# Hybrid attention and pooling layer: half of the output projection moved into the attention loop

## The chip, the cores and the metric

The kernel runs on one core of one Trainium2 chip. The metric is the device time of one execution in microseconds (us), a median over runs. The profile is that of one further execution; its span runs from the first to the last instruction on the core.

## The reference, cut to what matters

One layer over 2048 tokens of width 1024, float32. Half of the mixed width (512) is attention with eight heads of 64, the other half a pooled branch:

```
z = rmsnorm(x) @ w_in                    # q, k, v, u
att  = dilated_attention(q, k, v)        # 8 heads, three (window, dilation) patterns
pool = multiscale_pool(u)                # 4 groups of 128 channels
h = x + concat([att, pool]) @ w_out      # the output projection
h = h + (silu(gate) * val) @ w_down      # gated MLP, depthwise conv before the activation
h = h + sigmoid(rmsnorm(h) @ w_gate) * (p @ w_ple)
return rmsnorm(h)
```

So `h1 = x + att @ w_out[:512] + pool @ w_out[512:]`. The pooled half needs nothing of attention.

## The kernel before, in words

Everything is kept transposed: 128 channels on the partitions, tokens along the free axis, in four chunks of 512 tokens. A float32 product is made of float32r parts: each operand is split into a high part `hi` and the rest `lo`, and three matmuls (hi·hi, hi·lo, lo·hi) stand for one (`mm3`, lines 89 to 91). The program has four phases, one behind the other on TensorE: the input projection (`phase_project`, up to 397 us of the profile), attention (`phase_attention`, 397 to 724 us), the output projection (the first part of `phase_rest`, 724 to 926 us), and then the MLP and the gated embedding.

**Attention** runs 128 steps: 8 heads of 16 query tiles of 128 tokens, two heads being a pair. `CFG["ord"]` is the order in which each engine's work of a step is written: every pair is a stage and its lag in steps. `N` and `F` are the near and far scores on TensorE (lines 572 and 561), `nm` and `fm` bias and minimum on VectorE, `ne` and `fe` the exponentials on ScalarE, `T` the transposes of the weights (line 600), `h` and `l` their split on ScalarE and VectorE, `V` and `W` the products with the values, six steps later, into the one bank `o`. After two such steps the bank is emptied: `o` copies half of it on ScalarE (`ev`), `p` adds the other half on VectorE into `s1` or `s3` (line 660). Only then may the next `V` write it. `perm` is the order of the four query tiles in a group of four steps; a tile with a larger index has more far keys, and more blocks to transpose. Behind each of the first three pairs, `M` mixes its branches on GpSimd and its own DMA queue: weights are broadcast from DRAM (`wb`, line 891), products, split and stores of `mh` and `ml`. The order on TensorE, ScalarE, VectorE and GpSimd is as written; on SyncE (SP), which issues most loads, the planner sets it.

For each head, `load_qk` fetches queries and keys. An operand tile has 128 partitions, the 64 rows of a head twice: `qhh` holds the high part of q in both halves, `qll` the low part in both, `ks` the high part of k above its low part. These are six loads of 64 rows of 8 KB, 512 KB each:

```
for half in range(2):
    hs = slice(half * DH, half * DH + DH)
    loads.append((t.qhh[hs], g.qh[pr][rows]))
    loads.append((t.ks[hs], (g.kh if half == 0 else g.kl)[pr][rows]))
    loads.append((t.qll[hs], g.ql[pr][rows]))
```

The loads of head h+1 are issued one per step from the second step of head h on. PSUM has eight banks: one for near scores, two for far scores, two tiles of two banks for the transposes (`tp`), one for `o`.

**The output projection** goes chunk by chunk. For each of its 8 output tiles the sum over 8 row blocks of `w_out` is 24 matmuls of 512 columns; the pooled blocks are 4 to 7. Then the residual is added (line 1231, VectorE), `h1` is stored, and the square sum for the next norm is taken. In chunks 2 and 3 small pieces of the MLP's preparation, a list `todo`, are worked off on VectorE and ScalarE, one behind the matmuls of each row block and group of four tiles.

Of the kernel before, what the change touches and what calls it, by code (L numbers as in the profile page):

```python
# [43 lines left out]
CFG = {"tt": 2, "ee": 2, 'ord': [['B', 0], ['M', 0], ['N', 0], ['S', 1], ['o', 7], ['F', 0], ['h', 2], ['nm', 0], ['p', 7], ['fm', 0], ['l', 2], ['T', 1], ['V', 6], ['W', 6], ['ne', 0], ['fe', 0]], 'perm': [3, 2, 1, 0], 'fp': [[0], [1], [2], [3]], 'np': [[0, -1], [1], [2], [3]], 'm': [9, 10, 13, 4, 6, 7]}  # L44
# [125 lines left out]
def phase_project(tc, g, xT, w_in, pool_w, rcnt):  # L170
# [4 lines left out]
    with ExitStack() as ctx:  # L175
# [116 lines left out]
        for c, (t0, n) in enumerate(chunks):  # L292
# [3 lines left out]
            for gi, grp in enumerate((0, 1, 2, 3) if not final else (0, 1, 3, 2)):  # L296
# [58 lines left out]
                for j in range(nt):  # L355
# [16 lines left out]
                    elif grp == 1:  # L372
# [3 lines left out]
                        rdma(nc, residues(g.kh[j], t0, n), hi)  # L376
                        rdma(nc, residues(g.kl[j], t0, n), lo)
# [108 lines left out]
def phase_attention(tc, g, mx, near_b, far_b):  # L486
# [4 lines left out]
    NS = H * NQ  # L491
    with ExitStack() as ctx:
# [3 lines left out]
        ps_t = ctx.enter_context(tc.tile_pool(name="b_t", bufs=2, space=PSUM, reuse_waits="tile"))  # L496
        ps_o = ctx.enter_context(tc.tile_pool(name="b_o", bufs=1, space=PSUM, reuse_waits="tile"))

        heads, steps, groups, pairs = {}, {}, {}, {}

        def load_qk(h):
# [23 lines left out]
        def load_v(pr, which, q):  # L525

            v = sb.tile([P, 4, 2, P], F32R, tag=which, bufs=4 + (which == "v1"), name=f"{which}_{pr}_{q}")
# [5 lines left out]
        V_STEPS = {n: (("v3", "v1")[x], q) for x in range(2) for q, n in enumerate(((24, 28, 32, 36), (19, 30, 34, 38))[x])}  # L533

        def begin(s):
# [16 lines left out]
            st.tt = sb.tile([P, 768], F32, tag="tt", bufs=CFG["tt"], name="tt")  # L552
            st.ee = sb.tile([P, 768], F32, tag="ee", bufs=CFG["ee"], name="ee")

# [150 lines left out]
        def mix(s):  # L705
            for pr in range(NPAIR - 1):
# [9 lines left out]
                for c in range(NCH):  # L716
                    if d == CFG["m"][2] + CFG["m"][3] * c:
                        mix_fetch(nc, g, mx, nc.gpsimd, pr, pairs[pr], c)
                    if d == CFG["m"][2] + CFG["m"][3] * c + CFG["m"][4]:
                        mix_products(nc, g, mx, nc.gpsimd, pairs[pr], c)  # L720
                    if d == CFG["m"][2] + CFG["m"][3] * c + CFG["m"][5]:
                        mix_store(nc, g, mx, nc.gpsimd, nc.gpsimd, pr, pairs[pr], c)()

        near_bank = []
        sel = mx.tile([8, NCH, 2, DH], F32R, tag="sel", name="sel")
        for c in range(NCH):
            nc.vector.tensor_copy(sel[:, c], g.ident[:8, c : 8 : NCH, None].to_broadcast([8, 2, DH]))
        with tc.manual_schedule(engines=set(EN.values())):
            for dst, src in load_qk(0):
                rdma(nc, dst, src)  # L730
            for q in range(4):
# [5 lines left out]
                "T": turn, "h": high, "l": low, "V": values, "W": values_b, "S": stats, "M": mix, "o": fold, "p": folded, "B": begin  # L737
            }
            for s in range(NS + 10):
                if s < NS:  # L740
# [5 lines left out]
                    for pr in range(1, NPAIR):  # L746
                        if s - 2 * NQ * (pr - 1) in V_STEPS:
                            rdma(nc, *load_v(pr, *V_STEPS[s - 2 * NQ * (pr - 1)]))
                if s == NS + 2:
                    last_far(nc, g, mx, ps_t, pairs[NPAIR - 1])  # L750
                    pieces = pairs[NPAIR - 1].pieces = last_weights(nc, mx, pairs[NPAIR - 1])
                for nm, lag in CFG["ord"]:
                    if 0 <= s - lag < NS or nm == "M":
# [7 lines left out]
def mix_stats(nc, g, sb, psum, pr, pt):  # L761
# [8 lines left out]
    sy = sb.tile([16, CH], F32, tag="sy", name="sy")  # L770
# [23 lines left out]
def last_near(nc, g, sb, psum, pt):  # L794
# [9 lines left out]
    pt.near = [sb.tile([16, CH], F32, tag="sy", name="nr")[:8], sb.tile([P, CH], F32, tag="m3", bufs=1, name="nr")[:8]]  # L804
# [4 lines left out]
def last_far(nc, g, sb, psum, pt):  # L809
# [5 lines left out]
    pt.far = [sb.tile([8, CH], F32, tag="fr", bufs=2, name="fr") for _ in range(2)]  # L815
# [4 lines left out]
def last_weights(nc, sb, pt):  # L820

    both = (pt.near, pt.far)
    lo = sb.tile([P, CH], F32, tag="m1", bufs=1, name="lo")[:8]
# [71 lines left out]

# [1076 lines left out]
```

## Time and profile before

| | us |
|---|---|
| median of 3 runs (2460.84 to 2463.77) | 2463.16 |
| the profiled execution: its span | 2454.4 |
| time of the median run around that span | 8.8 |
| first near score to last near score (128 steps) | 397.7 to 706.4 |
| chunk 0 of the output projection | 724 to 800 |
| chunks 1 to 3 | 800 to 926 |

The trace names an instruction by engine, source line and tiles, `out<-in`. "PE" is TensorE, "DVE" VectorE, "ACT" ScalarE, "POOL" GpSimd; "PEld" is a weight load. The DMA share is the busy share of the core's 16 DMA engines. q0 is the queue that GpSimd issues to ("software_dynamic" in the profile), q1 that of SP ("hardware_dynamic").

### The profile page before, as it was taken

Reading aid. Unit: us, or ns where it says so; the run is one execution under the profiler, and the core shown is the slowest. Engines: PE = TensorE matmul, PEld = TensorE weight load, DVE = VectorE, ACT = ScalarE, POOL = GpSimd, SP = SyncE. Lnnn points to the kernel's source line nnn. Section 1 sums busy time; section 2 is a strip of 40 time slices with the busy share of each in tenths; the row PEclk is TensorE's granted clock in tenths of the full one; section 3 lists DMA queues with packets and bytes.
Section 4 is the critical chain, followed back from the end, with each engine's and each line's share of the span. In section 5 each row is a group of like instructions: output and inputs, shape, how many; then the busy total and the mean of one; then the engine's idle time right before and its main releaser. Section 6 shows DMA issues by size and latency. Waiting matters only on the chain.

```text
span 2454.4 us, 32544 instructions
## 1 busy us (share of the span) xinstructions
PE 2345.7 (96%) x11251; PEld 1970.6 (80%) x11251; DVE 1723.2 (70%) x2705; ACT 1146.1 (47%) x2055; POOL 547.3 (22%) x552
## 2 busy tenths in 40 slices
PE   8999999888879999999999999999999999999998
PEld 7888887787767887888888787788878888888888
DVE  6645437787774367999999989877766565755655
ACT  5423326787761125445445545444445444543332
POOL 3312221044340023344332366100020000000100
PEclk9999999898989999999999999999999999999999
DMA  7535448878747576456566778544388676654332
GB/s 240 175 133 185 146 153 249 178 173 193 181 142 260 189 253 202 161 187 211 192 197 219 260 275 272 197 145 142 125 287 287 226 255 206 215 176 158 125 100 91
DMA packets 248516, 476.06 MB, mean 194 GB/s; under 512 B 47744, under 2 KB 74176, under 8 KB 245280
## 3 DMA queue, kind: packets, MB, share of 16 engines
q1 hardware_dynamic: 199376, 385.20, 49.7%
q0 software_dynamic: 29328, 61.02, 7.4%
q10 hardware_dynamic: 19648, 27.77, 3.3%
q8 instruction: 88, 1.44, 0.3%
q14 instruction: 76, 0.62, 0.1%
HBM read 313.08 MB, written 160.73 MB: 193 GB/s over the span
## 4 chain that ended last, share of the span: by engine, by line
PE 73%; DVE 10%; DMA 7%; issue 4%; ACT 2%; POOL 0%; DVEq 0%; POOLq 0%; ACTq 0%; SPq 0%
PE ua L1319 15%; PE uc L1319 8%; PE dn L90 5%; PE dn L89 5%; PE dn L91 5%; PE ub L1319 4%; PE z L91 4%; PE z L89 4%; PE z L90 4%; PE o L89 2%; PE o L91 2%; PE o L90 2%; PE gp L89 2%; PE gp L90 2%; PE gp L91 2%
## 5 line engine op out<-in xcount | busy, mean ns | idle before, releaser
L90 PE MATMUL dn<-al,wu 128*128 128x512 f32 x616 | 240.1, 390 | 4.7 <-DVE al L85 4.7
L89 PE MATMUL dn<-ah,wu 128*128 128x512 f32 x616 | 240.1, 390 | 0.0
L91 PE MATMUL dn<-ah,wu 128*128 128x512 f32 x616 | 239.8, 389 | 0.0
L85 DVE TENSOR_TENSOR al<-ra,ah 128x512 fp32r<-128x512 f32 x154 | 105.8, 689 | 114.1 <-ACT ah L84 110.7
L89 PE MATMUL z<-hnh,wh 128*128 128x512 f32 (+1 forms) x480 | 169.9, 354 | 9.5 <-ACT hnh L252 6.0
L90 PE MATMUL z<-hnl,wh 128*128 128x512 f32 (+1 forms) x480 | 169.7, 354 | 3.4 <-DVE hnl L253 3.3
L91 PE MATMUL z<-hnh,wl 128*128 128x512 f32 (+1 forms) x480 | 169.6, 353 | 2.3 <-POOL wl L85 1.7
L84 ACT CAST ah<-ra 128x512 fp32r<-128x512 f32 x154 | 95.2, 621 | 148.2 <-PE dn L91 130.6
L90 PEld LDWEIGHTS dn<-al,wu 128*128 128x128 f32 x616 | 115.6, 188 | 30.0 <-DVE al L85 6.2
L85 DVE TENSOR_TENSOR wu<-ru,wu 128x1024 fp32r<-128x1024 f32 x88 | 136.5, 1551 | 2.4 <-ACT wu L84 2.4
L89 PEld LDWEIGHTS dn<-ah,wu 128*128 128x128 f32 x616 | 115.6, 188 | 24.3 <-ACT ah L84 0.2
L91 PEld LDWEIGHTS dn<-ah,wu 128*128 128x128 f32 x616 | 115.6, 188 | 23.9
L1319 PE MATMUL uc<-a22h,wu 128*128 128x512 f32 x352 | 116.9, 393 | 3.4 <-DVE uv L1342 3.4
L1319 PE MATMUL ua<-s1h,wu 128*128 128x512 f32 x352 | 115.8, 390 | 3.0 <-ACT ug L1546 3.0
L1319 PE MATMUL ub<-a12h,wu 128*128 128x512 f32 x352 | 117.0, 393 | 0.7 <-ACT a12h L1375 0.6
L1319 PE MATMUL ua<-s2h,wu 128*128 128x512 f32 x352 | 115.9, 390 | 0.9 <-ACT ug L1520 0.7
L1319 PE MATMUL ua<-s4h,wu 128*128 128x512 f32 x352 | 115.7, 389 | 0.5 <-ACT uv L1567 0.5
L1319 PE MATMUL uc<-s3h,wu 128*128 128x512 f32 x352 | 115.6, 389 | 0.0
L1319 PE MATMUL ua<-a11h,wu 128*128 128x512 f32 x352 | 115.5, 389 | 0.0
L85 DVE TENSOR_TENSOR wu<-rw,wu 128x512 fp32r<-128x512 f32 x149 | 101.0, 687 | 17.3 <-ACT wu L84 17.3
L89 PEld LDWEIGHTS z<-hnh,wh 128*128 128x128 f32 x480 | 94.0, 196 | 21.5 <-ACT hnh L252 6.0
L155 DVE TENSOR_TENSOR acc<-acc,sq 128x512 f32<-128x512 f32 (+1 forms) x125 | 81.1, 649 | 42.0 <-ACT sq L154 28.5
(336 smaller groups left out, 6670.3 us busy)
## 6 DMA issues: line engine op xcount, KB each, us to landing
ru<-in_w_up_dram SPq DMA_DIRECT2D x66, 512.0 KB, 4.1
wr<-in_w_in_dram SPq DMA_DIRECT2D x64, 256.0 KB, 4.2
rw<-in_w_down_dram SPq DMA_DIRECT2D x61, 256.0 KB, 4.0
nt<-h SPq DMA_DIRECT2D x56, 256.0 KB, 3.8
td<-t SPq DMA_DIRECT2D x22, 512.0 KB, 2.6
t<-td SPq DMA_DIRECT2D x22, 512.0 KB, 3.7
nt<-in_w_down_dram POOLq DMA_DIRECT2D x44, 256.0 KB, 5.4
ra<-oq0s SPq DMA_DIRECT2D x44, 256.0 KB, 3.9
```

The source lines that it names most:

```text
L84: nc.scalar.copy(hi, src)
L85: (low or nc.gpsimd).tensor_tensor(lo, src, fp(hi), op=ALU.subtract)
L89: nc.tensor.matmul(ps, wh, ah, start=first, stop=False, skip_group_check=again)
L90: nc.tensor.matmul(ps, wh, al, start=False, stop=False, skip_group_check=again)
L91: nc.tensor.matmul(ps, wl, ah, start=False, stop=last, skip_group_check=again)
L155: nc.vector.tensor_tensor(acc[:, :n], acc[:, :n], sq[:, :n], op=ALU.add)
L1319: nc.tensor.matmul(pst, x[:, ksl], y, start=first and k == 0 and n == 0, stop=k == HK - 1 and n == 2, skip_group_check=True)
```

## The change

The pooled half of chunks 1 to 3, 288 matmuls, moves into the attention loop, into steps 15 to 110. A part is one output tile of one chunk (24 parts), spread over four steps: four matmuls in each of the first three (`X`, line 780 of the new kernel), and in the fourth the addition of the residual on VectorE (`E`, line 788). SP fetches four 128x128 blocks of `w_out` for the next part (`xr`, 256 KB), the tile of `x` (`xx`), and stores the sum to `h1`; GpSimd splits the weights into `xh` and `xl`. The pooled activations of a chunk (`xa`, 2 MB) are loaded ahead. In the output projection chunks 1 to 3 then sum row blocks 0 to 3 alone and read `h1` in place of `x`, and two pieces of `todo` follow each row block instead of one.

The sums of `X` take one PSUM bank. `perm` alternates steps with many and with few transposes, and a step with few takes a one-bank tile `u`: `tp` then has three banks in all in place of four. Scores and exponentials share one tile (`tt` is `ee`), the products of `M` are written over `wb`, and one buffer of values goes. Six loads of a head become three: `kh` and `kl` lie in one DRAM tensor `kk`, and each load fills all 128 partitions from a source that is 2 x 64 rows of 8 KB, for q the same 64 rows twice.

```diff
-            loads = []
-            for half in range(2):
-                hs = slice(half * DH, half * DH + DH)
-                loads.append((t.qhh[hs], g.qh[pr][rows]))
-                loads.append((t.ks[hs], (g.kh if half == 0 else g.kl)[pr][rows]))
-                loads.append((t.qll[hs], g.ql[pr][rows]))
-            loads += [(t.fb, far_b[h]), (t.nb, near_b[h])]
-            return loads
+            both = lambda z: z[pr][None, rows].to_broadcast([2, DH, S])
+            return [
+                (t.qhh, both(g.qh)),
+                (t.ks.rearrange("p c r j -> p (c r j)"), g.kk[pr][:, rows].rearrange("a p c r j -> a p (c r j)")),
+                (t.qll, both(g.ql)),
+                (t.fb, far_b[h]),
+                (t.nb, near_b[h]),
+            ]
...
-            st.tp = ps_t.tile([P, 1024], F32, tag="t", name="tp")
+            if st.nf > 2:
+                st.tp = ps_t.tile([P, 1024], F32, tag="t", name="tp")
+            else:
+                st.tp = ps_t.tile([P, CH], F32, tag="u", name="tp")
...
+        def fill_loads(s):
+            u, j = divmod(s - FILL, 4)
...
+            if 0 <= u + 1 < len(parts) and j == 0:
+                held["raw"] = mx.tile([P, 4, P], F32, tag="xr", name="xr")
+                o = parts[u + 1][1]
+                nc.sync.dma_start(held["raw"], w_out[4 * P :, o * P : (o + 1) * P].rearrange("(k p) n -> p k n", p=P))
+            if 0 < u <= len(parts) and j == 0:
+                c, o = parts[u - 1]
+                nc.sync.dma_start(g.h1[o][:, c * CH : (c + 1) * CH], fills.pop(u - 1).x)
+            if 0 <= u < len(parts):
+                c, o = parts[u]
+                if j == 1:
+                    fl = fills[u]
+                    fl.x = mx.tile([P, CH], F32, tag="xx", bufs=2, name="xx")
+                    nc.sync.dma_start(fl.x, xT[o, :, c * CH : (c + 1) * CH])
...
+                if j == 2:
+                    hi = held["next"] = mx.tile([P, CH], F32R, tag="xh", bufs=2, name="xh")
+                    nc.gpsimd.tensor_copy(hi, raw)
+                if j == 3:
+                    hi, lo = held["next"], mx.tile([P, CH], F32R, tag="xl", name="xl")
+                    nc.gpsimd.tensor_tensor(lo, raw, fp(hi), op=ALU.subtract)
...
+            mine = [(k, w, a) for k in range(4) for w, a in ((hi, 0), (hi, 1), (lo, 0))]
+            for n, (k, w, a) in list(enumerate(mine))[4 * j : 4 * j + 4]:
+                nc.tensor.matmul(fills[u].ps, w[:, k * P : (k + 1) * P], acts[c, k][a], start=n == 0, stop=n == 11)
...
+            if 0 <= u < len(parts) and j == 3:
+                fl = fills[u]
+                nc.vector.tensor_tensor(fl.x, fl.ps, fl.x, op=ALU.add)
...
-            mix = {k: load_mix(c, k) for k in ks[:split_at]}
+            kc = ks if c == 0 else ks[4:]
+            mix = {k: load_mix(c, k) for k in kc[:split_at]}
...
-                    if todo:
-                        todo.pop(0)()
+                    for _ in range(2):
+                        if todo:
+                            todo.pop(0)()
...
-                    nc.sync.dma_start(x, xT[4 * grp + j, :, cs])
+                    nc.sync.dma_start(x, g.h1[4 * grp + j][:, cs] if c else xT[4 * grp + j, :, cs])
```

How the loads stand on SP where the fifth head's are issued; `qh`, `kh`, `kl` and `ql` are the DRAM tensors of q and k, the last figures the destination. Before:

```order
L56 DMA qhh_5290<-qh_83 64x2048
L56 DMA ks_5292<-kh_91 64x2048
L56 DMA qll_5291<-ql_87 64x2048
L56 DMA qhh_5290<-qh_83 64x2048
L56 DMA ks_5292<-kl_95 64x2048
L56 DMA qll_5291<-ql_87 64x2048
L56 DMA fb_5294<-in_far_b_dram 128x512
```

The same place in the changed kernel; `h_399` is a tile of `h1`:

```order
L56 DMA qhh_5458<-qh_83 128x1x2048
L56 DMA ks_5460<-kk_91 128x1x2048
L56 DMA qll_5459<-ql_87 128x1x2048
L743 DMA xr<-in_w_out_dram 128x4x128
L746 DMA h_399<-xx 128x512
L56 DMA fb_5462<-in_far_b_dram 128x512
L752 DMA xx<-in_xT_dram 128x512
```

The weights and the `x` tile of two parts now stand on SP's queue right behind the three loads of a head.

One step of attention on TensorE, near scores to values, where `V` begins to write the bank `o`. Before:

```order
L572 MATMUL sn<-ks_4018,qhh_4016 128x256
L573 MATMUL sn<-ks_4018,qll_4017 128x256
L561 MATMUL sf<-ks_4018,qhh_4016 128x512
L562 MATMUL sf<-ks_4018,qll_4017 128x512
L600 MATMUL tp<-ident,ee 128x128 x2
L628 MATMUL o<-pth,v_0_3_3998 128x256
```

In the changed kernel, a group later:

```order
L573 MATMUL sn<-ks_4407,qhh_4405 128x256
L574 MATMUL sn<-ks_4407,qll_4406 128x256
L562 MATMUL sf<-ks_4407,qhh_4405 128x512
L563 MATMUL sf<-ks_4407,qll_4406 128x512
L604 MATMUL tp<-ident,ee 128x128 x3
L780 MATMUL x<-xa1l,xh 128x512
L780 MATMUL x<-xa1h,xl 128x512
L780 MATMUL x<-xa2h,xh 128x512
L780 MATMUL x<-xa2l,xh 128x512
L632 MATMUL o<-pth,v_1_1_4956 128x256
```

The four matmuls stand between the transposes and the values.

VectorE in a fourth step of a part in the changed kernel; `ISA` is the fused bias and minimum:

```order
L621 TENSOR_TENSOR ptl<-tp,pth 128x384
L788 TENSOR_TENSOR xx<-x,xx 128x512
L578 ISA ee,st_3991<-sn,nb_4009 128x256
L578 ISA st_3991 128x1
L664 TENSOR_TENSOR s_3993<-o,ev 64x512
```

The addition of the residual, which needs the load of `xx`, stands ahead of the step's near minimum and of the addition that frees `o`; before, the split (`ptl`) was followed by that minimum directly.

More of the change, by code (lines that the diff above doesn't have):

```diff
@@ L525, in load_v @@
         def load_v(pr, which, q):
[L527 removed]
+            v = sb.tile([P, 4, 2, P], F32R, tag=which, bufs=4, name=f"{which}_{pr}_{q}")
             vals[pr, which, q] = v
@@ L719, in mix, with load_acts @@
                     if d == CFG["m"][2] + CFG["m"][3] * c + CFG["m"][4]:
-                        mix_products(nc, g, mx, nc.gpsimd, pairs[pr], c)
+                        mix_in_place(nc, nc.gpsimd, pairs[pr], c)
                     if d == CFG["m"][2] + CFG["m"][3] * c + CFG["m"][5]:
                         mix_store(nc, g, mx, nc.gpsimd, nc.gpsimd, pr, pairs[pr], c)()
+        parts = [(c, j) for c in range(1, NCH) for j in range(KD)]
+        acts, held, fills = {}, {}, {}
+        def load_acts(c, k):
+            acts[c, k] = [mx.tile([P, CH], F32R, tag=f"xa{k}{a}", name=f"xa{k}{a}") for a in "hl"]
+            for t, m in zip(acts[c, k], (g.mh, g.ml)):
+                rdma(nc, t, m[4 + k][:, c * CH : (c + 1) * CH])
@@ new lines, in fill @@
+        def fill(s):
+            u, j = divmod(s - FILL, 4)
+            if not 0 <= u < len(parts) or j == 3:
+                return
+            c, o = parts[u]
+            if j == 0:
+                fills[u] = Shared()
+                fills[u].ps = ps_x.tile([P, CH], F32, tag="x", name="x")
+            hi, lo = held[u]
+            mine = [(k, w, a) for k in range(4) for w, a in ((hi, 0), (hi, 1), (lo, 0))]
+            for n, (k, w, a) in list(enumerate(mine))[4 * j : 4 * j + 4]:
+                nc.tensor.matmul(fills[u].ps, w[:, k * P : (k + 1) * P], acts[c, k][a], start=n == 0, stop=n == 11)
+            if j == 2:
+                held.pop(u)
@@ L736, in phase_attention @@
                 "F": far_scores, "N": near_scores, "fm": far_max, "nm": near_max, "fe": far_exp, "ne": near_exp,
-                "T": turn, "h": high, "l": low, "V": values, "W": values_b, "S": stats, "M": mix, "o": fold, "p": folded, "B": begin
+                "T": turn, "h": high, "l": low, "V": values, "W": values_b, "S": stats, "M": mix, "X": fill, "E": fill_out, "o": fold, "p": folded, "B": begin
             }
@@ L748, in phase_attention @@
                             rdma(nc, *load_v(pr, *V_STEPS[s - 2 * NQ * (pr - 1)]))
+                fill_loads(s)
+                fill_split(s)
+                if s == NS:
+                    sel = mx.tile([P, CH], F32R, tag="xh", bufs=2, name="sel")[:8].rearrange("p (c e d) -> p c e d", c=NCH, e=2)
+                    for c in range(NCH):
+                        nc.vector.tensor_copy(sel[:, c], g.ident[:8, c : 8 : NCH, None].to_broadcast([8, 2, DH]))
                 if s == NS + 2:
@@ L803, in last_near @@
             )
-    pt.near = [sb.tile([16, CH], F32, tag="sy", name="nr")[:8], sb.tile([P, CH], F32, tag="m3", bufs=1, name="nr")[:8]]
+    pt.near = [sb.tile([P, CH], F32, tag=t, name="nr")[:8] for t in ("xl", "xa1l")]
     for a in range(2):
@@ L814, in last_far @@
             nc.tensor.transpose(out[:, r, :], pt.st3[:, r, a].rearrange("p e i -> p (e i)"), g.ident)
-    pt.far = [sb.tile([8, CH], F32, tag="fr", bufs=2, name="fr") for _ in range(2)]
+    pt.far = [sb.tile([P, CH], F32, tag=t, name="fr")[:8] for t in ("xa0h", "xa0l")]
     for a in range(2):
@@ L918, in mix_store @@
     cs = slice(c * CH, (c + 1) * CH)
-    hi = sb.tile([P, CH], F32R, tag="ah", bufs=3, name="ah")
-    lo = sb.tile([P, CH], F32R, tag="al", bufs=3, name="al")
+    if pr == NPAIR - 1 and c == NCH - 1:
+        hi, lo = (sb.tile([P, CH], F32R, tag=t, name=t) for t in ("xa3h", "xa3l"))
+    else:
+        hi = sb.tile([P, CH], F32R, tag="ah", bufs=2, name="ah")
+        lo = sb.tile([P, CH], F32R, tag="al", bufs=2, name="al")
     mix_split(nc, eng, pt, hi, lo)
@@ L1160, in step, with begin_both, wait @@
                 return [load] + [lambda x=x: (small[x](), small[x + 1]()) for x in range(0, 8, 2)]
-            out = [lambda: begin_one(c0), lambda: begin_one(c0 + 1)]
+            def begin_both():
+                for c in (c0, c0 + 1):
+                    dgs = spread_prep(nc, g, sb, g.pw[c])
+                    todo.insert(len(todo) - 4 * 5 - (c == c0), lambda c=c, dgs=dgs: spread_one(c, dgs))
+            def wait():
+                pass
+            if half:
+                out = [lambda: begin_one(c0), lambda: begin_one(c0 + 1)]
+            else:
+                out = [begin_both] + [wait] * 3
             for k in range(KD // 2):
@@ L1190, in one @@
                     todo.extend(prepare(0, np0, todo))
-            tk.later(4, one)
+            tk.later(2 if c == 1 else 4, one)
         for c in range(NCH):
```

57 lines of the change are left out of this document (34 added, 23 removed).

## The prediction

> **What bounds the kernel now.** I read the page's engine totals, then the stretches of the phases, then attention step by step, and last the DMA queues, since the change gives SP other loads. First the page, engine by engine: busy time, share of the span, instructions.
>
> ```profile
> PE 2345.7 (96%) x11251; PEld 1970.6 (80%) x11251; DVE 1723.2 (70%) x2705; ACT 1146.1 (47%) x2055; POOL 547.3 (22%) x552
> ```
>
> TensorE bounds the kernel, and the change adds and removes no matmul: it can only fill or open gaps of TensorE. Next the stretches that it touches: steps 15 to 110 of attention, chunk 1 of the output projection, chunks 2 and 3. Columns: length, busy time of each engine, granted clock, DMA share, GB/s. Then the near scores with which steps 15 and 111 begin, and those of two steps four apart.
>
> ```profile
> core 0: us, PE busy (x) PEld busy (x) DVE busy (x) ACT busy (x) POOL busy (x), PEclk, DMA share, GB/s
> 428.35:671.85 243.50, 203.76 (x1246) 183.85 (x1246) 187.06 (x559) 193.16 (x533) 75.21 (x79) 0.93 0.79 183
> 800.00:842.00 42.00, 42.00 (x188) 34.81 (x189) 11.51 (x19) 5.29 (x9) 1.04 (x1) 1.00 0.64 206
> 842.00:926.00 84.00, 83.42 (x376) 68.85 (x375) 51.73 (x75) 24.12 (x39) 16.41 (x12) 1.00 0.65 216
> ...
> 428.35 0.28 PE L572 MATMUL sn<-ks,qhh 128*128 128x256 f32 x1
> ...
> 671.85 0.28 PE L572 MATMUL sn<-ks,qhh 128*128 128x256 f32 x1
> ...
> 440.04 0.33 PE L572 MATMUL sn<-ks,qhh 128*128 128x256 f32 x1
> ...
> 448.25 0.33 PE L572 MATMUL sn<-ks,qhh 128*128 128x256 f32 x1
> ```
>
> Chunks 1 to 3 run TensorE without a gap; attention does not. The 96 steps took 243.5 us, 24 groups of four; an undisturbed group took 8.21 us, so 46.5 us are disturbances. What TensorE waited for in these steps (total, times, longest):
>
> ```profile
> PE o L628 <- DVE s L660: 20.5, 24, 5.3
> PE o L642 <- DVE s L660: 10.7, 23, 1.0
> ...
> PE sn L573 <- DMA qll<-ql: 2.6, 1, 2.6
> ```
>
> It is the wait for the emptied bank `o`: 31.2 us in all, 1.3 us a group. So the room is small: the moved matmuls take longer than this (below), and the gap between them and the waits must be paid in attention.
>
> **The change, part by part.** *The matmuls out of the projection.* A row of the chain prices twelve 512-column matmuls, and VectorE's residual addition has its own row:
>
> ```profile
> 964.24 2.72 PE uc L1319 x12
> ...
> L1231 DVE TENSOR_TENSOR xc<-o,xc x32: 679/686/692, 784.0 to 924.7; 128x512 f32<-128x512 f32 x32
> ```
>
> 288 are 24 x 2.72 = 65.3 us, all on the path there: minus 65.3. The cover of VectorE's work goes with them. In chunks 2 and 3 TensorE keeps 84.0 - 43.5 = 40.5 us, VectorE still has 51.7: 11 us become visible, at the bank's release or at the MLP's start. Bounds: 0, if that start waits for nothing of it; 17, if nothing of VectorE's late start in chunk 2 is caught up. I take 11. Net: minus 54.
>
> *The same matmuls in attention.* A group becomes 8.21 + 2.72 us less what they cover. `X` stands ahead of `V` in the step of L628's wait (20.5 us), not in that of L642's, where `E` stands. In an undisturbed group I take 0.4 us as covered: 10.53 us, 24 x 10.53 = 252.7. Of the 46.5 us of disturbances half, 23, since longer steps give the loads that cause them more time: 276, or plus 32 against 243.5. Bounds 252.7 (plus 9) and 299 (plus 56). VectorE (187 us + 24 x 0.69) and ScalarE (193) have room in 276 us, so `E` costs nothing while `xx` is there; if it is late, the near minimum, the freeing of `o` and the next `V` are late behind it.
>
> *GpSimd's splits.* Casting and subtracting 128x512:
>
> ```profile
> 694.35 0.61 POOL L913 CAST ah<-m 128x512 fp32r<-128x512 f32 x1
> 695.04 1.28 POOL L914 TENSOR_TENSOR al<-m,ah 128x512 fp32r<-128x512 f32 x1
> ...
> POOL wb L891 <- issue: 20.5, 3, 8.9
> POOL m L902 <- DMA wb<-wd: 19.5, 5, 13.4
> ```
>
> 1.9 us a group, hidden outside the mixing. In it GpSimd has about 9.0 us for one chunk, so 10.9 against 10.5: 0.4 us over some ten groups, 4 us, inside the bounds above. Its waits (40 us in two rows) were free; now the next part's weights queue behind them: rival D.
>
> *Nothing taken for:* one `tp` of each size (alternating steps reuse a buffer after two steps, as before); the minimum written into `ee` (the transposes that free it stand ahead of the same step's scores on TensorE); products over `wb`, four value buffers, the later `S`, and `sel` (VectorE has 56 us free here; without it, under 1 us each); moved loads and stores of `x`, `h1` and `xa` (25 MB over 276 us, 91 GB/s beside 183, under the 401 below).
>
> *The loads of a head.* This decides. First transfers of one size on one queue, from 688 to 704 us, when little else ran (KB each, median us from issue to landing); then the DMA share in single stretches.
>
> ```profile
> ml<-al POOLq DMA_DIRECT2D x2, 256.0 KB, 3.3
> wb<-wd POOLq DMA_DIRECT2D x2, 256.0 KB, 8.9
> ...
> 684.00:687.00 3.00, 3.00 (x24) 2.98 (x23) 2.35 (x9) 2.62 (x8) 2.82 (x3) 1.00 0.24 90
> 692.40:693.30 0.90, 0.90 (x7) 0.90 (x7) 0.90 (x3) 0.51 (x3) 0.82 (x2) 1.00 0.11 46
> 694.50:696.50 2.00, 1.88 (x15) 1.64 (x13) 1.38 (x5) 1.95 (x6) 1.92 (x3) 1.00 0.30 105
> 697.60:698.10 0.50, 0.50 (x5) 0.50 (x4) 0.45 (x1) 0.50 (x3) 0.50 (x1) 1.00 1.00 401
> 511.00:523.00 12.00, 10.87 (x74) 9.91 (x74) 10.63 (x33) 10.99 (x32) 10.84 (x11) 1.00 0.95 195
> ```
>
> A plain 256 KB store fills all engines (share 1.00, 401 GB/s). `wb` has the same size and takes three times as long: with one left in flight the share is 0.11 of 16, 1.8 engines, at 46 GB/s, 26 GB/s each. Its source is 2 rows broadcast to 64 partitions each: an outermost step of 2. It ran on two engines. The merged loads have just that form, 2 x 64 rows onto 128 partitions; the six old ones, 64 rows, used all engines though at half rate (511 to 523: 0.95, 195 GB/s). No SP load of before has an outermost step under 16, so its queue's behaviour isn't shown; bounds are 2 engines and 16. I take 2, since the form is nearest to `wb`. Price of one, 1.049 MB: at 2 x 26 GB/s 20.2 us (22.4 at the 23.4 GB/s an engine of 684 to 687), three 60.5; at 401 GB/s 2.6, three 7.8.
>
> Which two is the next question. Two `wb` in flight took 0.30 x 16 = 4.8 engines, so that GpSimd's take turns. The page names that queue "software_dynamic" and SP's "hardware_dynamic"; a turn needs a kept state, and I take the same two each time for SP as likelier. The Trainium skill ("DMA: Bandwidth & Descriptors", section "Why a DMA increments its semaphore by 16 and not by 1") says that the largest number up to 16 that divides the outermost counts of both sides sets the engines, on both kinds of queue, and that SP's queue takes the lowest-numbered ones while GpSimd's moves on. The trace agrees for GpSimd's queue (1.8 engines); no run here shows it for SP's. By it the sum is that of the same two, by turns that of rival B.
>
> With the same two, three loads of a head pass one behind the other, and what SP issues behind them has a sixteenth of its bytes on each of these engines, so it lands when they are through. SP's rows at the start, and the first and last near score:
>
> ```profile
> 358.17 0.51 SPq L56 DMA_DIRECT2D qhh<-qh  x1
> ...
> 402.49 0.38 SPq L56 DMA_DIRECT2D v<-vf  x1
> ...
> L572 PE MATMUL sn<-ks,qhh x128: 222/332/562, 397.7 to 706.4; 128*128 128x256 f32 x120, 128*128 128x128 f32 x8
> ```
>
> Head 0: 358.2 + 60.5 + 2.5 (landing; the 3.3 us of `ml` less its data) = 421 in place of 397.7. The values, 4.2 MB, of which a sixteenth at 26 GB/s is 10 us: 429. Head 1: 489. `xa`, the first weights and the biases, 2.75 MB: 6.6 us, 496; landing and GpSimd's split: the first `X`, step 15, at 500 instead of 428. From then a head costs this: its loads are issued at about its first step, the residual tile for `E` in its seventh step stands behind them and comes 60.5 + 2.5 + 1 = 64 us later, the weights with it; the ten steps left at 10.53/4 take 26.3. That is 90.3 us. Step 16 at 502.6, step 32 at 502.6 + 64 + 26.3 = 593, step 112 at 593 + 5 x 90.3 = 1044, step 111 at 1042 instead of 671.85: plus 370. The rest of attention has no fills and no loads of heads.
>
> *Sum:* 2454.4 + 370 - 54 = 2770 us of span, and 8.8 around it (the median against the span of the profiled execution): 2779, said as 2780. Its own range: 22.4 us a load adds 9 a head at eight heads, 70 or so; loads that overlap the steps better, or steps of 2.4 us, take off up to 80. 2700 to 2870.
>
> **The rivals.** *B, two engines but in turns.* Each load 20.2 us beside the others; a head's seventh step comes 25 us after its first instead of 15.8, plus 9 x 6, the start plus 17: with the 32 and -54 of above 2463 + 32 - 54 + 71 = 2512 (2475 to 2540). For it: 4.8 engines on GpSimd's queue.
>
> *C, all 16 engines, the other sign.* SP's queue splits the 128 destination rows. Three loads take 7.8 us instead of 15 at 195 GB/s, the weights are in time, and attention costs plus 32: 2463 + 32 - 54 = 2441, between 2418 and 2465 by the bounds above. For it: every load of SP in the trace uses 16 engines. Against it: none has this form. It decides from about 10 us a load on: a part's weights have 10.5 us from issue to use, less 1.9 for the split.
>
> *D, 16 engines, but GpSimd paces attention.* Its waits in the mixing (rows above, with smaller ones some 55 us over twelve chunks, 4.6 each) hold up ten parts: 2441 + 46 = 2487. Against it: longer steps give `wb` more time.
>
> **How the numbers follow.** A change of 0.2% (5 us) is about what a measurement of this kernel can tell from none. The same two engines 0.70; B 0.10; C 0.15, of which 0.02 within 5 us of before; D 0.05. Faster 0.13, same 0.02, slower 0.85. The predicted time is that of the likeliest, 2780. The range must hold eight in ten: it takes its own case, B and D, 2475 to 2880, and leaves out C.
>
> **What would show it.** Right: stretches with a DMA share near 0.12 and about 50 GB/s, some 60 us at each of heads 1 to 6; landings of `qhh`, `ks` and `qll` of 20, 40 and 60 us; TensorE and VectorE waiting for `xl`, `xh` and `xx` once a head; the last near score near 1080; chunks 1 to 3 in some 72 us. Wrong: landings under 10 us and steps of 2.6 us (C), 20 us each side by side (B), or long waits for `xl` behind GpSimd's `wb` alone (D). A group of four steps without a wait over 11 us would refute the price of the fills; chunks 1 to 3 over 80 us that of the cover.

## The result and the profile after

The changed kernel takes 2848.16 us (median of 4 runs, 2844.12 to 2853.38) beside 2462.00 of the kernel before (4 runs, 2460.66 to 2463.77): a ratio of 1.156, 95% interval 1.154 to 1.158. The profiled execution took 2844.12 us, its span is 2842.3. One of the four executions of run e8 below took 4637.1 us, for a reason that no trace shows, and is left out of its figures.

TensorE's busy time is almost that of before; what grew is the time in which it stands still:

```profile
PE 2359.9 (83%) x11251; PEld 1985.4 (70%) x11251; DVE 1741.9 (61%) x2729; ACT 1145.0 (40%) x2055; POOL 594.7 (21%) x600
```

The near scores with which steps 15, 16, 111 and 127 begin (start, us):

```profile
467.11 0.28 PE L573 MATMUL sn<-ks,qhh 128*128 128x256 f32 x1
...
520.02 0.52 PE L573 MATMUL sn<-ks,qhh 128*128 128x256 f32 x1
...
1112.16 0.28 PE L573 MATMUL sn<-ks,qhh 128*128 128x256 f32 x1
...
1146.26 0.28 PE L573 MATMUL sn<-ks,qhh 128*128 128x256 f32 x1
```

Step 111 begins at 1112.2 where it began at 671.85: plus 440.3. From the last near score to the end the program takes 2842.3 - 1146.3 = 1696.0 us, before 2454.4 - 706.4 = 1748.0: minus 52.0. These two make the result: 440.3 - 52.0 = 388, and the spans differ by 387.9.

One stall, in head 3, shows what the 440 are. First SP's issues (start, duration), then the first instruction of VectorE and of TensorE behind the stall, with the wait in brackets, then a stretch inside it (length, busy times, granted clock, DMA share, GB/s):

```profile
709.70 0.51 SPq L56 DMA_DIRECT2D qhh<-qh  x1
711.05 0.69 SPq L56 DMA_DIRECT2D ks<-kk  x1
711.79 19.70 SPq L56 DMA_DIRECT2D qll<-ql  x1
731.62 5.24 SPq L743 DMA_DIRECT2D xr<-in_w_out_dram  x1
736.97 27.67 SPq L746 DMA_DIRECT2D h<-xx  x1
764.68 2.41 SPq L56 DMA_DIRECT2D fb<-in_far_b_dram  x1
767.43 2.15 SPq L752 DMA_DIRECT2D xx<-in_xT_dram  x1
```

```profile
780.67 0.69 DVE L788 TENSOR_TENSOR xx<-x,xx 128x512 f32<-128x512 f32 x1 [53.92 <-DMA xx<-in_xT_dram]
```

```profile
782.35 0.79 PE L646 MATMUL o<-pth,v 128*128 128x512 f32 x1 [53.17 <-DVE s L664]
```

```profile
745.00:764.00 19.00, 0.00 (x0) 0.00 (x0) 0.00 (x0) 0.00 (x0) 0.00 (x0) 0.50 0.13 54
```

For 19 us no engine works. 0.13 of 16 DMA engines are busy, 2.1, at 54 GB/s: at this rate one merged load of 1.049 MB takes 19.4 us, three 58. SP's next issues are held up while they are queued: the issue of a store to `h1`, 0.5 us in the median, takes 27.7. The residual `xx` is issued 57.7 us behind `qhh`, and VectorE, which works in order, can begin `E` with it 13 us later; the emptying of bank `o` is behind it, and TensorE waits for that. Over steps 0 to 111 (total, times, longest):

```profile
POOL xh L763 <- DMA xr<-in_w_out_dram: 495.0, 22, 105.3
...
PE o L646 <- DVE s L664: 205.1, 26, 53.2
DVE xx L788 <- DMA xx<-in_xT_dram: 139.1, 3, 53.9
...
ACT ev L663 <- DMA ks<-kk: 103.8, 3, 37.0
```

In the even heads the wait is split in two: first ScalarE, in order too, is held between two small loads that it issues for the mixing, and the copy that empties half of `o` stands behind them. The view names the landing of `ks` as the end of that wait. In head 2 (start, duration, wait in brackets):

```profile
631.92 0.39 ACTq L853 DMA_DIRECT2D sn<-std  x1
653.07 0.37 ACTq L857 DMA_DIRECT2D sf<-stf  x1
653.48 0.58 ACT L663 COPY ev<-o 64x512 f32<-64x512 f32 x1 [32.43 <-DMA ks<-kk]
```

Last, the projection: first the stretch that answers to 800 to 926 us before, then the wait of TensorE at the start of the MLP, before and after:

```profile
1240.00:1318.00 78.00, 64.08 (x275) 51.42 (x274) 57.95 (x90) 25.89 (x46) 19.89 (x13) 0.92 0.86 273
...
927.50 0.50 PE L1319 MATMUL ua<-s2h,wu 128*128 128x512 f32 x1 [0.68 <-ACT ug L1520]
...
1318.75 0.79 PE L1410 MATMUL ua<-s2h,wu 128*128 128x512 f32 x1 [7.53 <-ACT ug L1611]
```

The stretch takes 78 us in place of 126. Both leave out the beginning of chunk 1, whose first matmul starts at 788.6 us before and at 1228.4 now. From there to the end of the wait shown it is 138.9 us before and 90.4 now: 48.5 less, where the moved matmuls alone are 65.3.

### The profile page after: what moved, and what is told of

It is laid out like the page before. It is cut to its first block, busy times and chain, and to the rows that moved or that the text cites. A ratio compares the mean times of both kernels' runs of the same rounds, so it can differ in the third digit from the quotient of the medians.

```text
span 2842.3 us, 32655 instructions
## 1 busy us (share of the span) xinstructions
PE 2359.9 (83%) x11251; PEld 1985.4 (70%) x11251; DVE 1741.9 (61%) x2729; ACT 1145.0 (40%) x2055; POOL 594.7 (21%) x600
## 4 chain that ended last, share of the span: by engine, by line
PE 47%; DVE 5%; DMA 3%; issue 3%; ACT 1%; POOL 0%; SPq 0%; DVEq 0%; POOLq 0%; ACTq 0%
PE ua L1410 14%; PE uc L1410 7%; PE dn L90 5%; PE dn L91 5%; PE dn L89 5%; PE ub L1410 4%; PE gp L89 2%; PE gp L91 2%; PE gp L90 2%; DVE wu L85 1%; DMA oq1s<-x 1%; PE o L91 1%; PE o L89 1%; PE o L90 1%; DMA nt<-h 0%
## 5 line engine op out<-in xcount | busy, mean ns | idle before, releaser
L646 PE MATMUL o<-pth,v 128*128 128x512 f32 (+3 forms) x128 | 46.4, 372 | 208.7 <-DVE s L664 208.7
L646 PEld LDWEIGHTS o<-pth,v 128*128 128x128 f32 x128 | 27.0, 211 | 219.1 <-DVE s L664 216.1
L590 ACT ACTIVATE ee<-ee,st 128x256 f32<-128x256 f32 (+1 forms) x128 | 64.4, 503 | 247.5 <-DVE st L578 245.2
L578 DVE CUSTOM_DVE_ANT_0 ee<-sn,nb 128x256 f32<-128x256 f32 (+1 forms) x128 | 53.1, 415 | 156.4 <-PE sn L574 126.8
L788 DVE TENSOR_TENSOR xx<-x,xx 128x512 f32<-128x512 f32 x24 | 16.6, 692 | 214.0 <-DMA xx<-in_xT_dram 139.1
L632 PE MATMUL o<-pth,v 128*128 128x256 f32 (+1 forms) x152 | 41.1, 294 | 104.2 <-DVE s L664 104.2
L663 ACT COPY ev<-o 64x512 f32<-64x512 f32 x64 | 37.2, 581 | 218.6 <-DMA ks<-kk 103.8
L763 POOL CAST xh<-xr 128x512 fp32r<-128x512 f32 x24 | 14.7, 611 | 495.0 <-DMA xr<-in_w_out_dram 495.0
```

Of the source, the lines that this page charges most:

```text
L578: nc.vector.tensor_tensor_reduce(st.tt[:, st.ns], st.nv, st.t.nb[:, 256 - st.wn :], 1.0, BIG, ALU.add, ALU.min, st.nm1)
L590: nc.scalar.activation(st.ee[:, st.ns], st.tt[:, st.ns], AF.Exp, bias=st.nm1, scale=-1.0, accum_out=st.d1)
L632: nc.tensor.matmul(gr.o[:, m0 * P : (m1 + 1) * P], vals[gi // 8, "v1", kt // 4][:, kt % 4, gi // 4 % 2, :], pt[:, b0 : b1 + 1 : 4, :], sta ...
L646: nc.tensor.matmul(gr.o[:, kb * P :], vals[gi // 8, "v3", gi % 4][:, kb, gi // 4 % 2, :], pt[:, 6 * kb + 2 : 18 + kb : 5, :], start=first, ...
L663: nc.scalar.copy(ev[mine], o[other])
L788: nc.vector.tensor_tensor(fl.x, fl.ps, fl.x, op=ALU.add)
```

## The experiments

Theory: the merged loads run on two of the sixteen DMA engines because their source has an outermost step of 2, and everything behind them on SP waits. Rivals: the size of the loads or the doubled reading; the fills, through GpSimd and the order on VectorE; or engines taken in turns. The table gathers what the near scores and spans of the runs give (us): steps 15 to 111 (the parts lie there), and from the last near score to the end (the projection and what follows). The rows for it stand below where a verdict rests on them. Ratios are to the kernel before on the same chip.

| kernel | time | ratio (95%) | steps 15 to 111 | last near score to end |
|---|---|---|---|---|
| before | 2462.0 | | 243.5 | 1748.0 |
| changed | 2848.2 | 1.156 (1.154 to 1.158) | 645.0 | 1696.0 |
| e1 changed, six old loads | 2504.1 | 1.017 (1.015 to 1.019) | 341.5 | 1701.6 |
| e2 before, merged loads | 2740.5 | 1.113 (1.111 to 1.115) | 468.6 | 1741.8 |
| e3 changed, rows outermost | 2460.6 | 0.999 (0.998 to 1.000) | 292.8 | 1699.0 |
| e4 before, merged loads on GpSimd | 2576.8 | 1.047 (1.044 to 1.049) | 307.6 | 1750.5 |
| e5 changed, 62 rows | 2846.0 | 1.155 (1.152 to 1.158) | 641.5 | 1699.0 |
| e6 before, rows outermost | 2434.0 | 0.988 (0.987 to 0.990) | 216.8 | 1750.7 |
| e7 e3 and early residual | 2450.7 | 0.995 (0.993 to 0.997) | 288.5 | 1698.1 |
| e8 e7, chunk 1 alone | 2427.2 | 0.986 (0.983 to 0.988) | 238.0 | 1724.9 |
| e9 before, alternate partitions | 2429.6 | 0.989 (0.988 to 0.991) | 217.2 | 1745.7 |
| e10 e8, four steps later | 2424.2 | 0.986 (0.985 to 0.988) | 238.0 | 1720.4 |
| e11 e7, weights once | 2437.8 | 0.992 (0.991 to 0.994) | 275.7 | 1701.7 |
| e12 changed, 60 rows | 2508.8 | 1.019 (1.015 to 1.024) | 342.1 | 1702.3 |

The kernel before, measured beside each group of runs, had a median of 2456.8 beside e9 to e11 and of 2463.4 to 2464.6 beside the others. So times compare within a group (e1 to e4, e5 to e8, e9 to e11), and ratios across groups.

**e1, the six old loads.**

```
-            both = lambda z: z[pr][None, rows].to_broadcast([2, DH, S])
...
+            for half in range(2):
+                hs = slice(half * DH, half * DH + DH)
+                loads.append((t.qhh[hs], g.qh[pr][rows]))
+                loads.append((t.ks[hs], g.kk[pr][half, rows]))
+                loads.append((t.qll[hs], g.ql[pr][rows]))
```

> The changed kernel with the six 64-row loads of a head (512 KB each) in place of the three merged ones; fills, banks, buffers and projection stay as changed. Theory 1 (the merged loads run on two of the sixteen DMA engines, and everything SP issues behind them waits): the flat stretches at 54 GB/s go, no wait of TensorE in attention is longer than about 6 us, steps 15 to 111 take some 276 us in place of 645, and the time is 2441 (2418 to 2465): before, plus 32 for the fills, less 54 in the projection. Rival (GpSimd's splits and the fills' own transfers pace attention, the merged loads only add to it): waits of 5 to 13 us for xl behind wb in the mixing stay, and the time is 2487 or more.

2504.1: the merged loads cost 344 us of the 386. But the waits did not fall to what the prediction's case C had (2441). The groups of four steps that begin at 52, 84 and 100 still lose 11 to 13 us each, and step 15, where the first part begins, takes 15 us in place of 2. The rival's number (2487 or more) came, but not its cause: TensorE waited once for the split weights (10.7 us, the first part), and VectorE 43.5 us in eight waits for `xx`, which stands behind the six loads on SP.

**e2, the merged loads alone.**

```
-            for half in range(2):
...
-                loads.append((t.ks[hs], (g.kh if half == 0 else g.kl)[pr][rows]))
...
+            both = lambda z: z[pr][None, rows].to_broadcast([2, DH, S])
+            return [
+                (t.qhh, both(g.qh)),
...
```

> The kernel before with nothing changed but the loads of a head: three merged ones of 1024 KB with an outermost step of 2 in the source, on SP. Theory 1, the same two engines each time: a head's loads take 3 x 19.4 = 58 us in a row (1.049 MB at the 54 GB/s of the changed kernel's flat stretches) and a head cannot start under some 62 us after the one before, in place of 38.6; 7 x 24 = 165, plus 23 at the start, plus 5 to 10 a head for half-clock steps behind each stall: 2690 (2640 to 2740), with no fills at all. Rival, two engines in turns: the three pass side by side in 20 us and are hidden behind a head, only the start pays: 2480. Rival, the loads are harmless alone and only the fills behind them make them cost: 2463 to 2480.

```profile
500.00:513.00 13.00, 2.54 (x8) 1.87 (x9) 1.55 (x4) 0.60 (x2) 0.00 (x0) 0.50 0.13 52
```

```profile
PE sn L573 <- DMA qll<-ql: 169.5, 8, 28.0
```

2740.5, just past the upper end of what was expected: with no fills, each head waits for its own `qll`, eight times, 169.5 us. A head takes 62 to 83 us, in place of 33 to 48 before. The same 0.13 and 52 GB/s are there, and the rivals (hidden behind a head; harmless without fills) are out.

**e3, rows outermost.** The order of the 128 rows of a contraction is free as long as keys and queries share it; so the two copies of a row can stand side by side.

```
-            both = lambda z: z[pr][None, rows].to_broadcast([2, DH, S])
+            def both(z):
+                v = z[pr][rows].rearrange("(g r) c -> g r c", g=64)
+                return v[:, None].to_broadcast([64, 2, DH // 64, S])
...
-                (t.ks.rearrange("p c r j -> p (c r j)"), g.kk[pr][:, rows].rearrange("a p c r j -> a p (c r j)")),
...
+                    g.kk[pr][:, rows].rearrange("a (g p) c r j -> g a p (c r j)", g=64),
```

> The changed kernel with one edit: the two copies of a head's row stand side by side on the partitions (2p and 2p+1) in place of 64 apart, so that the source's steps are 64 rows outermost and 2 within; still three loads of 1024 KB, 128 partitions, the same rows read twice. Theory 1 (the outermost step sets the number of engines): all sixteen engines, a load in 3 to 5 us, and the time is that of the six old loads or a little less: 2435 (2415 to 2465). Rival (the size of the loads, or that the same rows are read twice, makes them slow): 2800 to 2850 as changed.

Landings between 425 and 475 us (KB, median us), and the near scores of steps 15, 111 and 127:

```profile
qhh<-qh SPq DMA_DIRECT2D x1, 1024.0 KB, 6.6
ks<-kk SPq DMA_DIRECT2D x1, 1024.0 KB, 5.8
qll<-ql SPq DMA_DIRECT2D x1, 1024.0 KB, 7.7
```

```profile
428.92 0.28 PE L579 MATMUL sn<-ks,qhh 128*128 128x256 f32 x1
...
721.71 0.28 PE L579 MATMUL sn<-ks,qhh 128*128 128x256 f32 x1
...
755.82 0.28 PE L579 MATMUL sn<-ks,qhh 128*128 128x256 f32 x1
```

Same bytes, same size, same rows read twice, another order of the steps: 2460.6, the whole loss of 386 us is gone. The order of the steps is the cause. What is left of the change is nothing: plus 49.3 us in attention (292.8 against 243.5), minus 49.0 behind it. And it is 44 us faster than with the six old loads, which neither theory had.

**e4, the merged loads on GpSimd's queue.**

```
+            def qdma(dst, src):
+                if dst.dtype == F32R:
+                    nc.gpsimd.dma_start(fp(dst), fp(src))
+                else:
+                    rdma(nc, dst, src)
```

> The kernel before with the three merged loads (outermost step of 2) issued on GpSimd's queue in place of SP's. Theory 1 (two engines each, but GpSimd's queue takes turns, as two wb in flight took 4.8 engines): three loads of a head pass side by side, six engines, about 160 GB/s, some 20 us in all, hidden behind a head of 33 us; the start pays about 17, and GpSimd some 3 us a head for the issues: 2485 (2465 to 2520). Rival (two engines and in a row on any queue): 2690 as on SP.

```profile
qhh<-qh POOLq DMA_DIRECT2D x7, 1024.0 KB, 29.0
ks<-kk POOLq DMA_DIRECT2D x7, 1024.0 KB, 31.7
qll<-ql POOLq DMA_DIRECT2D x7, 1024.0 KB, 30.5
```

```profile
476.00:486.00 10.00, 9.32 (x64) 8.65 (x64) 8.72 (x28) 9.36 (x26) 0.00 (x0) 1.00 0.47 77
```

2576.8. Neither number was right, the mechanism of the first was: three loads issued within 2 us land together after some 30 us, not at 20, 40 and 60, and the share is 0.47, 7.5 engines. In the trace 6.05 of these carry the 8 KB rows of the three loads and 1.46 carry packets of 4 bytes. So here GpSimd's queue took two other engines for each load. But a row of 8 KB takes 0.65 us on the mean in this stretch, where it took 0.31 in the stretch of 19 us above, and a load 30 us, not 20; why wasn't tried. The first is issued at 402.7 (358 on SP), behind GpSimd's own stores of the input projection, and the first near score begins at 438.2.

**e5, 62 rows, and e12, 60 rows,** with the rows outermost as in e3 but each load cut in two:

```
+            for a, b in ((0, 62), (62, 64)):      # e12: ((0, 60), (60, 64))
+                ps = slice(2 * a, 2 * b)
+                loads += [(t.qhh[ps], both(g.qh, a, b)), (kd[ps], keys[a:b]), (t.qll[ps], both(g.ql, a, b))]
```

> The changed kernel with rows outermost as in the run before (two copies side by side on the partitions), but each merged load cut in two: rows 0 to 61 onto 124 partitions (1016 KB) and rows 62 and 63 onto four (32 KB). Theory 1, by the divisor (the largest number up to 16 that divides the outermost counts of both sides, here 62 and 124, so 2): two engines again, the flat stretches at some 54 GB/s are back and the time is that of the changed kernel, 2848 (2810 to 2870). Rival (a small outermost count is what limits the engines, 62 rows are enough for sixteen): as with 64 rows, 2460 to 2475 with the three loads more.

> As the run with 62 rows, but each merged load is cut at row 60: rows 0 to 59 onto 120 partitions (960 KB) and rows 60 to 63 onto eight (64 KB). Theory 1, the divisor (60 and 120 have 15 in common, the small load 4): fifteen engines, no flat stretches at 54 GB/s, and the time is that of the uncut loads with rows outermost or a little more, 2465 (2455 to 2485). Rival (it was the cut itself, a load of fewer than all the rows, or the small load beside it, that put the 62 rows on two engines): 2840 as with 62 rows.

A stretch of e5, and one of e12 in which head loads pass:

```profile
730.00:750.00 20.00, 0.00 (x0) 0.00 (x0) 0.00 (x0) 0.00 (x0) 0.00 (x0) 0.57 0.13 52
```

```profile
444.00:450.00 6.00, 5.87 (x20) 4.46 (x20) 2.37 (x6) 2.51 (x7) 1.01 (x1) 0.56 1.01 235
```

62 rows: 2846.0, 0.13 of 16 again. 60 rows: 2508.8, no such stretch. Neither a small outermost count nor the cut as such does it; the largest number up to 16 that divides 62 and 124 is 2, for 60 and 120 it is 15. The Trainium skill ("DMA: Bandwidth & Descriptors", section "Why a DMA increments its semaphore by 16 and not by 1") says that the number of engines is the largest number up to 16 that divides the outermost counts of both sides, on SP's queue as on GpSimd's. With 2, 62 and 64 the trace of SP's queue agrees (2.1, 2.1 and 16 engines); with 60 the trace can't tell 15 from 16, since other loads run beside. And e12 missed its number by 44 us: the engines are busy (1.01) but move 235 GB/s, while the three loads of 64 rows in e6 (below) moved 424. The stretch of e12 also holds weight loads in packets of 512 bytes, but the head's rows themselves are slow: 8 KB take 0.54 us on the mean in it, 0.31 in e6. Why 60 rows go at little over half the rate was not tried further and stays open.

**e6, the kernel before with rows outermost, and e9, with its six loads on alternate partitions.**

```
e6: the three loads of e3 in the kernel before
e9: -                hs = slice(half * DH, half * DH + DH)
    +                hs = slice(half, P, 2)
```

> The kernel before with nothing changed but the loads of a head: three merged ones with rows outermost, no fills. Theory 1 (the six old loads hold the other transfers up at half rate; in the kernel with fills that cost 44 us): the groups of four steps that lost 4 to 7 us behind head loads lose less, the 46.5 us of disturbances fall by 10 to 20, and the time is 2450 (2440 to 2458). Rival (before, nothing urgent stands behind the head loads; its disturbances come from the mixing alone): 2462, no change.

> The kernel before with nothing changed but where the six loads of a head land: still 64 rows of 8 KB each, 512 KB, but on every second partition (even for one copy, odd for the other) in place of partitions 0 to 63 and 64 to 127. Theory 1 (a load that fills only one half of the partitions gets half the rate: 195 GB/s at a share of 0.95 against 424 GB/s at 1.02 for 128): spread over all partitions, the six loads run at some 400 GB/s and the time is that of the merged loads with rows outermost, 2434 (2430 to 2442). Rival (the size of 512 KB, or 64 rows a load, sets the rate): still some 200 GB/s and 2463.

Near scores of steps 15, 111 and 127 of e6, then a stretch of head loads in e6 and in e9:

```profile
430.50 0.28 PE L578 MATMUL sn<-ks,qhh 128*128 128x256 f32 x1
...
647.29 0.28 PE L578 MATMUL sn<-ks,qhh 128*128 128x256 f32 x1
...
681.86 0.28 PE L578 MATMUL sn<-ks,qhh 128*128 128x256 f32 x1
```

```profile
434.00:438.00 4.00, 3.93 (x29) 3.67 (x29) 3.33 (x11) 3.70 (x11) 0.00 (x0) 1.00 1.02 424
```

```profile
504.00:512.00 8.00, 7.64 (x51) 7.10 (x51) 6.89 (x22) 7.55 (x22) 7.78 (x9) 1.00 0.98 325
```

e6: 2434.0, 30 us faster than before on the same chip and under the expected 2450 (2440 to 2458): steps 15 to 111 lose 26.7 us (243.5 to 216.8). Six groups of four steps that had lost 3 to 6 us each lose nothing of it now. e9 leaves size, rows and number of loads as they were and gives the same 217.2; its ratio (0.989) is e6's (0.988), and its time of 2429.6, just under the expected 2430 to 2442, goes with a kernel before that was 7 us faster there too. A row of 8 KB took 0.64 us on the mean in the kernel before (511 to 523 us), 0.31 in e6 and 0.38 in e9, in the stretches shown. So what cost the kernel before 27 us was that each load filled one half of the partitions (195 GB/s at a share of 0.95, against 325 to 424 at 0.98 to 1.02 over all of them). The Trainium skill ("SBUF — State Buffer", section "Door 1: The DMA port swizzle (why `[64,N]` ≈ `[32,N]`)") says that the rate depends on how many of 16 ports the partitions reach, and that partitions 0 to 63 reach only half; e9 agrees.

**e7, the residual fetched earlier:** in the fourth step of the part before, four steps ahead of its use in place of two (the expectation below says six).

```
-                if j == 1:   fl.x = ...; nc.sync.dma_start(fl.x, xT[o, :, ...])
+            if 0 <= u + 1 < len(parts) and j == 3:   fills[u + 1].x = ...; nc.sync.dma_start(fills[u + 1].x, ...)
```

> The changed kernel with rows outermost, and the residual tile xx of a part fetched two steps earlier (ten steps' halves: six steps ahead of its use in place of two). Theory 1 (where head loads fill the engines, xx lands after E is due; VectorE waits in order, bank o is emptied late and the next product with the values waits 2.7 to 3.5 us, after which the clock is lower for a while): the waits of VectorE for xx (9.5 us in 3) go, TensorE's waits for o fall from 19.8 to some 10, steps 15 to 111 take some 282 us in place of 292.8, the time is 2448 (2442 to 2455). Rival (the waits are the mixing's work on VectorE and the full DMA engines, and move on to xr or xa): 2460, no change.

TensorE's wait for the bank in e3, then in e7:

```profile
PE o L652 <- DVE s L670: 19.8, 21, 3.5
```

```profile
PE o L652 <- DVE s L670: 10.3, 24, 1.8
```

2450.7 against e3's 2460.6. The wait fell as told, by 9.5 us; of it 4.3 us show in the steps 15 to 111 (288.5). The two were measured on different chips; the spans of their traces differ by 4.9.

**e8, chunk 1 alone, and e10, four steps later.**

```
-        parts = [(c, j) for c in range(1, NCH) for j in range(KD)]
+        parts = [(1, j) for j in range(KD)]
-            kc = ks if c == 0 else ks[4:]
+            kc = ks[4:] if c == 1 else ks
e10: -    FILL, ACTS = 15, ...
     +    FILL, ACTS = 19, ...
```

> As the run with the early residual, but only the 8 parts of chunk 1 are computed in attention (steps 15 to 46); chunks 2 and 3 of the projection are as before the change, with one piece of preparation behind each row block. Theory 1 (in chunks 2 and 3 the cover of VectorE's work is what is lost, chunk 1 has none to lose): the projection gives back the full 8 x 2.72 = 21.8 us, a part costs attention 2.24 us and some disturbance, 8 x 2.24 + 3 = 21: within 3 us of the same kernel without fills. Rival (the projection gives back less in every chunk, some 0.75 of it): 5 us slower than the kernel without fills, and a third of the way to the kernel with all 24 parts.

> As the run with chunk 1 alone, begun four steps later (step 19 in place of 15). Theory 1 (the first part waits 3.3 us for its weights, which stand behind the values, the second head's loads and the pooled activations; that wait is in no later part): the group of steps 12 to 15 loses 5 us less, and the time is 2425 (2422 to 2427). Rival (the wait moves along, or the last part meets the mixing in the third head): 2429, no change.

Near scores of steps 15, 111 and 127 of e8:

```profile
428.32 0.28 PE L579 MATMUL sn<-ks,qhh 128*128 128x256 f32 x1
...
666.36 0.28 PE L579 MATMUL sn<-ks,qhh 128*128 128x256 f32 x1
...
700.45 0.28 PE L579 MATMUL sn<-ks,qhh 128*128 128x256 f32 x1
```

e8's three other executions took 2425.4 to 2430.1, those of e6 on the same chip 2432.9 to 2436.7. Eight parts cost attention 238.0 - 216.8 = 21.2 us, as expected. Behind attention, kernels without fills take 1741.8 to 1750.7 us (mean 1747.3 of five), with chunk 1 moved 1720.4 and 1724.9 (mean 1722.7), with all three 1696.0 to 1702.3 (mean 1699.7 of seven). So chunk 1 gives back some 25 us. Of these 21.8 are its matmuls: from the first matmul of chunk 1 to the first of chunk 2 it is 44.5 us before and 22.7 in e8. The other 3 are less than the 9 us by which the kernels without fills differ. Chunks 2 and 3 together give back 23.0 for 16 parts, 1.4 us a part in place of 2.72. There the cover is lost, as theory 1 said; the changed kernel's wait of 7.53 us at the start of the MLP, 0.68 before, is a part of it.

e10 has the same 238.0: the first part's wait went (the groups at 12 and 16 are 7.4 us shorter), others came from step 36 on. So the rival had the mechanism, the wait moves along. That 2424.2 lies in theory 1's range is luck: the kernel before, too, was 7 us faster there, and the ratio is e8's. The best version here is e8 or e10, 1.4% faster than before; 1.2 of it is the order of the loads. The rest, some 6 us beside e6 (e8) and beside e9 (e10), is more than the matmuls moved explain (21.8 gained, 21.2 paid).

**e11, the weights once.**

```
-            if 0 <= u + 1 < len(parts) and j == 0:   held["raw"] = ...; nc.sync.dma_start(held["raw"], w_out[...])
+            if u + 1 == 0 and j == 0:                held["raw"] = ...        # the splits likewise
-            hi, lo = held[u]
+            hi, lo = held[0]
```

It leaves out 23 of the 24 weight loads and their splits, so that all output tiles but the first are computed with the wrong weights; it shows time alone.

> As the run with the early residual and all 24 parts, but the weights of the first part are used for all: 23 loads of 256 KB and GpSimd's 46 casts and subtractions are left out (so is their part of the result). Theory 1 (GpSimd's mixing and the splits hold each other up: the groups of the mixing, steps 40 to 51, 68 to 79 and 100 to 107, cost 3 to 5 us over the 1.9 of an undisturbed one): those groups fall to some 11 us, minus 15 in all, 2435 (2430 to 2442). Rival (these groups are long because VectorE, ScalarE and the DMA engines have the mixing's work beside E): 2449, no change.

```profile
429.75 0.29 PE L579 MATMUL sn<-ks,qhh 128*128 128x256 f32 x1
...
705.46 0.28 PE L579 MATMUL sn<-ks,qhh 128*128 128x256 f32 x1
```

Steps 15 to 111 lose 12.7 us (288.5 to 275.7): the groups that begin at 68, 72 and 40 fall from 14.7, 13.3 and 13.3 us to 10.6, 11.3 and 11.3. So GpSimd's and the queues' share is real and about what theory 1 had. But those at 44, 48, 76 and 80 stay at 12 to 14. There the next chunk's `xa` are loaded, into buffers that the last part has only just left, and TensorE waits 5.2 us for them in three waits; that was in neither theory. The times come from two chips; by the ratios, whose intervals overlap, e11 is some 6 us faster than e7, so that not all of the 12.7 us of the traces is shown in the time.

## Why the prediction was right

The likeliest case of the forecast held, 2780 for the same two engines, loads one behind the other and the queue behind them. The range of 2475 to 2880 would have held B and D too; what bears the mechanism out are the traces and e2, e3 and e5. Point by point:

- *Two engines for SP's loads.* Shown by e3 and e5: the outermost step alone takes 386 us away or brings them back. Price of a load 20.2 us, measured 19.4 (1.049 MB at 54 GB/s).
- *The same two each time (0.70), not turns (B).* Shown by the flat 0.13 with three loads queued. The 4.8 engines that spoke for B are a matter of GpSimd's queue, where e4 shows three loads on six. Of the 4.8, 0.8 were a fetch of instructions, so that two `wb` held four.
- *Step 111 plus 370.* Measured plus 440, the largest miss. 17 of it are the start: step 16 at 520.0, not 502.6; SP could issue the last of the pooled activations only at 512, where the sum had them landed at 496. 52 are the heads: from step 16 to step 112 a head took (1113.8 - 520.0) / 6 = 99 us, not 90.3. The term for the residual was 64 us behind `qhh`; in head 3 it came at 71. The sum had 2.5 us for its landing; SP issued it 57.7 us behind, and it was there 13 us later. The granted clock after each stall (0.5 in the stretch above) and the mixing's own waits in even heads (102 to 107 us a head, 90 to 97 in the odd ones) were in no term.
- *What waits and in which order (`E`, then `o`, then the next `V`)* came as told, by the rows of head 3. The order's reason was incomplete: what stood behind was held back already at its issue. For the split weights TensorE waited only in the first parts (57.1 us in two waits), not once a head.
- *The projection, minus 54:* minus 52.0 behind the last near score, in part by luck. The projection itself gave back 48.5 of the 65.3 us, so that 17 us of cover were lost, the upper bound and not the 11 taken; the other 3.5 came in the MLP and were in no term. The stretch of chunks 1 to 3 took 78 us where some 72 were told.
- *The fills, plus 32 (bounds 9 and 56).* e3 shows them with good loads: plus 49. The undisturbed group came out at 10.45 to 10.48 where 10.53 was told, but by luck: the 8.21 us taken for a group before is the shortest from step 15 on, and the same four groups (from steps 20, 24, 56 and 88) took 8.49 to 8.66 in e6, so that twelve matmuls cost 1.8 to 2.0 us and some 0.8 were covered, not 0.4. Half of the "46.5 us of disturbances" was to go, but in e3 292.8 - 24 x 10.47 = 42 remain. e6 shows what the 46.5 were: 27 came from the old loads' half rate, and the other 20, counted from 8.21, are in e6 too. Against the kernel without that, the 24 parts of e3 cost 76 us, not 32, for 49 returned.
- *The 8.8 us around the span.* In the profiled execution of the changed kernel 1.8 us lie around its span. The 8.8 was a median less the span of another execution, and so mostly the difference between executions.
- *Case C, 2441,* was mispriced though it didn't happen: 2460.6 with all engines, at the upper end of its bounds, and 2504 with the six old loads. Rival D's waits are at most some 13 us (e11, which leaves out the weight loads as well), not 46.

## What to carry to other kernels

Before a load is merged or broadcast, look at the outermost count on both sides. It decided here, and not the bytes, how many DMA engines worked: 2 or 62 rows outermost gave two, 64 gave all, and with two everything behind on the queue waited. Let every load reach all partitions, whole or alternating: loads that filled one half of them ran at half rate. And work moved into a stage that TensorE nearly fills costs nearly its full time there. The 8 parts of chunk 1 cost 21.2 us and gave back their 21.8; all 24 parts cost 72 us (e7), and the 16 of chunks 2 and 3 gave back 23.

## What the runs showed of the hardware beyond that

- SP's issue of a DMA took longer while loads on two engines were queued: 0.3 us in the median, 19.7 and 27.7 in head 3, and 43.2 at the start, where the issue of one bias load (256 KB, 0.65 us in the kernel before) stands behind the three loads of head 0:

```profile
362.63 43.19 SPq L56 DMA_DIRECT2D fb<-in_far_b_dram  x1
```

- Six 64-row loads kept the engines' share at 0.95 at 195 GB/s, three loads with rows outermost at 1.02 and 424 GB/s: a high share was no sign of a high rate.
- The same form of load took 19.4 us on SP's queue and some 30 on GpSimd's, three in flight.
